# Expert matmuls of a two-layer MoE trunk: three fp32r passes over split weights, or plain float32 on 32-column tiles

## The chip, the cores and the metric

The kernel runs on one core of one Trainium2 chip. The metric is the device time of one execution in microseconds (us), the median of several runs.

## The reference, cut to what matters

A trunk of two layers over 512 tokens of width 1024. Each layer has a mixer (a state-space and pooling mixer in layer 0, a stick-breaking attention in layer 1), a layer norm, and then a mixture of 16 SwiGLU experts, of which each token uses two, beside a gated projection of an extra input:

```python
def grouped_moe(x, router_w, router_bias, w1, w3, w2):
    ...
    gates = jnp.sum(jax.nn.one_hot(idx, N_EXPERTS, dtype=F32) * w[..., None], axis=1)
    h = jax.nn.silu(jnp.einsum('td,edf->etf', xt, w1)) * jnp.einsum('td,edf->etf', xt, w3)
    h = h * gates.T[:, :, None].astype(h.dtype)
    y = jnp.einsum('etf,efd->td', h, w2)

def reference(...):
    for i in range(DEPTH):
        ...
        x = layer_norm(DEEPNORM_ALPHA * x + mix, ln_mix_g[i], ln_mix_b[i])
        ple = (p[i] @ ple_w_proj[i]) * jax.nn.sigmoid(x @ ple_w_gate[i])
        ffn = grouped_moe(x, router_w, router_bias, moe_w1[i], moe_w3[i], moe_w2[i])
        x = layer_norm(DEEPNORM_ALPHA * x + ffn + ple, ln_ffn_g[i], ln_ffn_b[i])
```

Per layer and expert, `w1` and `w3` are 1024 x 512 and `w2` is 512 x 1024, all float32.

## The kernel before, in words

The program runs in four stages: mixer 0, the expert layer 0, mixer 1 (attention), the expert layer 1. The change is in the expert layers, `ffn`, and in the helpers that load and split weights, which the mixers use too.

Each expert works on a list of at most 96 tokens (`CAP`). GpSimd gathers their rows from memory (`gather`, L936) and scatters the results back (`scatter`, L942). Per expert, six loads of 1 MB come through SP's queue (L107): two halves (of 512 rows) each of w1 and w3, and two halves (of 512 columns) of w2. `plan` lists all loads of the program in their order of use; `prefetch` issues them as far as `LA` loads ahead, into `NR` = 17 slots of 8 KB per partition (tag `raw`), which also hold the tokens `g`, the transposed activations and other tiles. A load puts row k*128 + p of the weights on partition p, so that each run of contiguous bytes is one row of 512 numbers, 2 KB.

A weight tile isn't multiplied as loaded. `weights` splits it (L84, L85): ScalarE copies a 128 x 1024 piece to the fp32r type as `w_0h` or `w_2h`, VectorE subtracts that copy from the original and gives `w_0l` or `w_2l`. These pairs live in a ring of 5 and 6 tiles. `mm3` then makes three matmuls for each product: high tokens with high weights (L89), high with low (L90), low with high (L91). The tokens (96 columns) are the stationary operand, 512 weight columns move. An expert has 24 such products, so 72 matmuls.

The order of an expert's work is written out in the loop over e. `up` for the next expert is cut in two halves of the contraction; between them stand the end of this expert and the load of the expert after the next one:

```python
            sg = act(hh)
            hh = [self.bank("A", "pA"), self.bank("A", "pA")]
            up(gn, hh, 0, 0)
            sT = turn(sg)
            up(gn, hh, 0, 1)
            ysb = self.half4("ysb")
            for h, py in down(sT):
                nc.scalar.activation(ysb[:CAP, h], py, AF.Copy)
            scatter(e, ysb)
```

`act` makes Silu on ScalarE (L1002) and the product on VectorE (L1003). `turn` transposes the result on TensorE (L1010) and splits it into `sT`. `down` multiplies by w2 into two PSUM banks `pB`, one after the other, and `load_g` transposes the tokens of a coming expert (L985) and splits them into `g`. After experts 3, 6 and 10 (`GATES`) a piece of the gated projection is put in. After the loop, the last expert's act, turn and down run with no other `up` beside them, and then each token's two results are added up by matmuls (L1068, L1071). A scheduler may move instructions of one engine against each other where their data allow it; the order of instructions that it leaves is shown below.

Of the kernel before, what the change touches and what calls it, by code (L numbers as in the profile page):

```python
# [7 lines left out]
F32 = mybir.dt.float32  # L8
F32R = mybir.dt.float32r
# [3 lines left out]
OP = mybir.AluOpType  # L13
# [5 lines left out]
KB = 8  # L19
# [1 line left out]
EPS = 1e-5  # L21
NE = 16
CAP = 96
NR = 17
RING = 6
NH = 5
GATES = (-1, 3, 6, 10)
OVER = 12
# [12 lines left out]
class Trunk:  # L41
# [51 lines left out]
    def plan(self, ap, k, n):  # L93
        self.queue.append((ap, k, n))
        return len(self.queue) - 1

    def prefetch(self, upto, parts=1):
        while self.loaded < min(upto, len(self.queue)):
            ap, k, n = self.queue[self.loaded]
            if k * n <= 512:  # L100
                t = self.sb.tile([128, 512], F32, tag="wp", bufs=1, name=f"raw{self.loaded}")
            else:
                t = self.slot(f"raw{self.loaded}")
            dst = t[:, :k * n].rearrange("p (k n) -> p k n", k=k)
            src = ap.rearrange("(k p) n -> p k n", p=128)
            for a in range(0, k, k // parts):
                self.nc.sync.dma_start(dst[:, a:a + k // parts], src[:, a:a + k // parts])  # L107
            self.raws[self.loaded] = t
            self.loaded += 1

    def weights(self, ahead, pool=False):
        i = self.used
        self.prefetch(i + 1 + ahead)
        self.used += 1
        ap, k, n = self.queue[i]
# [360 lines left out]
    def plain(self, ahead):  # L476
        i = self.used
        self.prefetch(i + 1 + ahead)
        self.used += 1
        ap, k, n = self.queue[i]  # L480
        return self.raws.pop(i)[:, :k * n].rearrange("p (k n) -> p k n", k=k)

    def mixer0(self):
# [433 lines left out]
    def ffn(self, layer, last):  # L917
# [34 lines left out]
            for k in range(2):  # L952
                self.mm3(p, (pT[:, 0, k, ts], pT[:, 1, k, ts]), w[k], k == 0, k == 1)

        LA = 6

        def gate(c):
            w = self.weights(LA, c < ng)
# [18 lines left out]
            gate(c)  # L977

        def load_g(e):
            g = self.slot(f"g{layer}_{e}", F32R)[:, :2 * KB * CAP].rearrange("p (a k t) -> p a k t", a=2, k=KB)  # L980
            for hf in range(2):
                p = self.bank("T", "pT")[:, :4 * CAP]
                for k in range(4):
                    kb = hf * 4 + k
# [21 lines left out]
        def turn(t):  # L1006
            sT = self.half4("sT", F32R)[:, :8 * CAP].rearrange("p (a k t) -> p a k t", a=2, k=4)
            p = self.bank("T", "pT")[:, :4 * CAP]
            for k in range(4):
                nc.tensor.transpose(p[:, k * CAP:(k + 1) * CAP], t[:CAP, k * 128:(k + 1) * 128], self.ident[:CAP, :CAP])  # L1010
            self.split(sT[:, 0], sT[:, 1], p.rearrange("p (k t) -> p k t", k=4))
            return sT

        def down(sT):
            for nh in range(2):
                w = self.weights(LA)
                py = self.bank("B", "pB")[:CAP]
                for k in range(4):
                    self.mm3(py, (sT[:, 0, k], sT[:, 1, k]), w[k], k == 0, k == 3)
                yield slice(nh * 512, (nh + 1) * 512), py  # L1020

        g = load_g(0)
        hh = [self.bank("A", "pA"), self.bank("A", "pA")]
        up(g, hh, 0, 0)
        up(g, hh, 0, 1)
        gn = load_g(1)
        up(g, hh, 1, 0)
        up(g, hh, 1, 1)
        for e in range(NE - 1):
            LA = 6 if e < 13 else 3  # L1030
            sg = act(hh)
            hh = [self.bank("A", "pA"), self.bank("A", "pA")]
# [17 lines left out]
            up(g, hh, 1, 0)  # L1050
            up(g, hh, 1, 1)
# [6 lines left out]
        for h, py in down(turn(act(hh))):  # L1058
            nc.scalar.activation(yl[:CAP, 0, h], py, AF.Copy, scale=self.gs[:CAP])
            v.scalar_tensor_tensor(yl[:CAP, 1, h], py, self.gs[:CAP], yl[:CAP, 0, h].bitcast(F32),  # L1060
                                   op0=OP.mult, op1=OP.subtract)
        st = self.cp.tile([128, NT, 12], F32, tag="st", bufs=2, name=f"st{layer}f")
        for i in range(NT):
# [129 lines left out]
    def plan_ffn(self, layer):  # L1193
# [7 lines left out]

        def up(e, kh):
            for n in ("moe_w1", "moe_w3"):
                self.plan(I[n][layer, e, kh * 512:(kh + 1) * 512, :], 4, 512)

        for c in range(GATES.count(-1)):
            gate(c)
# [2 lines left out]
        for e in range(NE):  # L1210
            if e + 1 < NE:
                up(e + 1, 0)
            for nh in range(2):
                self.plan(I["moe_w2"][layer, e, :, nh * 512:(nh + 1) * 512], 4, 512)
            if e in GATES:
                gate(GATES.index(e))
            if e + 1 < NE:
# [62 lines left out]
```

## Time and profile before

| | us |
|---|---|
| median of 3 runs | 1280.6 (1278.77 to 1281.57) |
| span of the profiled execution | 1278.0 |
| mixer 0 and routing, about 0 to 230 us of the span | 230 |
| expert layer 0, to the end of its loop | 230 to 550 |
| its end | 550 to 580 |
| mixer 1, routing | 580 to 900 |
| expert layer 1, its loop and its end | 900 to 1278 |

No time apart from the span is given for the profiled execution itself; the runs lie 0.8 to 3.6 us above the span, the median 2.6 us. A view in groups gives the busy time of each engine, a view in windows the same for stretches, the timeline every instruction in order, the waits what an engine waited for. The mean clock of TensorE over the span was 0.971 of full speed.

### The profile page before, as it was taken

What the parts mean: (1) busy time and instruction counts of PE and PEld (TensorE: products, weight loads), DVE (VectorE), ACT (ScalarE), POOL (GpSimd) and SP (SyncE); (2) the same over time, 40 slices, a digit from 0 to 9 for tenths busy, and PEclk for the clock granted to TensorE, in tenths of its full rate; (3) what the DMA queues carried; (4) which work ended last, traced back from release to release, by engine and by line L of the source; (5) the groups of instructions that cost most, each with busy time, mean ns of one, the idle gap of its engine ahead of it and who ended that gap; (6) DMA issues with size and microseconds to landing.
All of it is one profiled execution on the core that took longest, in us unless ns stands there. A gap on an engine that the chain in (4) does not pass through costs nothing. (4 is left out here: it accounts for less than half of the span.)

```text
span 1278.0 us, 17420 instructions
## 1 busy us (share of the span) xinstructions
PE 1191.0 (93%) x6511; PEld 910.8 (71%) x6511; DVE 982.7 (77%) x1358; ACT 748.4 (59%) x1043; POOL 180.5 (14%) x166
## 2 busy tenths in 40 slices
PE   6588998999999999997999999998999999999895
PEld 5467787778787786755877877787777778787662
DVE  7999678896969968766477376868797887969676
ACT  4123522886868868752465445612687786868761
POOL 5820031110000100003000000022111000010104
PEclk9888999999999999998999999998899999999898
DMA  8116463898998998971113023443599797999842
GB/s 236 58 50 211 153 229 123 278 365 304 339 340 303 365 337 317 344 273 34 34 32 101 1 67 121 161 148 124 189 353 373 266 370 275 364 340 356 314 189 89
DMA packets 158164, 285.12 MB, mean 223 GB/s; under 512 B 19584, under 2 KB 43664, under 8 KB 157008
## 3 DMA queue, kind: packets, MB, share of 16 engines
q1 hardware_dynamic: 143760, 256.56, 57.5%
q0 software_dynamic: 9568, 25.19, 5.8%
q10 hardware_dynamic: 4736, 2.10, 0.6%
q8 instruction: 55, 0.90, 0.3%
q14 instruction: 45, 0.37, 0.1%
HBM read 272.02 MB, written 20.19 MB: 229 GB/s over the span
## 5 line engine op out<-in xcount | busy, mean ns | idle before, releaser
L85 DVE TENSOR_TENSOR w_0l<-raw,w_0h 128x1024 fp32r<-128x1024 f32 (+1 forms) x231 | 281.3, 1219 | 68.2 <-ACT w_0h L84 59.8
L84 ACT ACTIVATE w_0h<-raw 128x1024 fp32r<-128x1024 f32 (+1 forms) x233 | 242.8, 1042 | 78.7 <-PE pG L91 37.8
L85 DVE TENSOR_TENSOR w_2l<-raw,w_2h 128x1024 fp32r<-128x1024 f32 x205 | 249.9, 1219 | 20.7 <-ACT w_2h L84 20.4
L84 ACT ACTIVATE w_2h<-raw 128x1024 fp32r<-128x1024 f32 x205 | 216.6, 1056 | 43.2 <-PE pA L91 34.1
L89 PE MATMUL pA<-w_0h,g 128*96 128x512 f32 x256 | 106.0, 414 | 0.0
L90 PE MATMUL pA<-w_0l,g 128*96 128x512 f32 x256 | 102.4, 400 | 0.0
L91 PE MATMUL pA<-w_2h,g 128*96 128x512 f32 x256 | 101.8, 398 | 0.0
L91 PE MATMUL pA<-w_0h,g 128*96 128x512 f32 x256 | 101.7, 397 | 0.0
L89 PE MATMUL pA<-w_2h,g 128*96 128x512 f32 x256 | 101.4, 396 | 0.0
L942 POOL DMA_INDIRECT yd<-ysb,ixm x30 | 32.2, 1075 | 488.1 <-ACT ysb L1038 488.1
L90 PE MATMUL pA<-w_2l,g 128*96 128x512 f32 x256 | 101.2, 395 | 0.0
L90 PEld LDWEIGHTS pA<-w_2l,g 128*96 128x96 f32 x256 | 41.8, 163 | 18.2
L91 PEld LDWEIGHTS pA<-w_0h,g 128*96 128x96 f32 x256 | 41.7, 163 | 17.9
L91 PEld LDWEIGHTS pA<-w_2h,g 128*96 128x96 f32 x256 | 41.6, 162 | 18.1
L89 PEld LDWEIGHTS pA<-w_2h,g 128*96 128x96 f32 x256 | 41.6, 163 | 18.0
L936 POOL DMA_INDIRECT xg<-xd,ixm x32 | 34.1, 1067 | 143.2 <-PE pT L985 98.6
L90 PEld LDWEIGHTS pA<-w_0l,g 128*96 128x96 f32 x256 | 42.4, 166 | 15.5 <-DVE w_0l L85 1.1
L89 PEld LDWEIGHTS pA<-w_0h,g 128*96 128x96 f32 x256 | 42.2, 165 | 14.5 <-ACT g L84 0.5
L89 PE MATMUL pB<-w_0h,sT 128*96 128x512 f32 x128 | 50.6, 396 | 1.2 <-ACT sT L84 1.2
L91 PE MATMUL pB<-w_0h,sT 128*96 128x512 f32 x128 | 51.4, 401 | 0.0
L90 PE MATMUL pB<-w_0l,sT 128*96 128x512 f32 x128 | 50.7, 396 | 0.4 <-DVE w_0l L85 0.4
L89 PE MATMUL pB<-w_2h,sT 128*96 128x512 f32 x128 | 50.8, 397 | 0.0
(439 smaller groups left out, 2918.5 us busy)
## 6 DMA issues: line engine op xcount, KB each, us to landing
raw<-in_moe_w_dram SPq DMA_DIRECT2D x192, 1024.0 KB
raw<-in_sb_w_qkv_dram SPq DMA_DIRECT2D x12, 1024.0 KB
raw<-in_ple_w_gate_dram SPq DMA_DIRECT2D x8, 1024.0 KB
yt<-yd SPq DMA_DIRECT2D x8, 1024.0 KB
raw<-in_ab_w_out_dram SPq DMA_DIRECT2D x4, 1024.0 KB
xd<-x0r POOLq DMA_DIRECT2D x8, 512.0 KB, 3.4
raw<-in_sb_w_out_dram SPq DMA_DIRECT2D x4, 1024.0 KB
raw<-in_ab_w_in_dram SPq DMA_DIRECT2D x3, 1024.0 KB
```

The lines of the kernel that those rows point to most:

```text
L84: return (self.nc.scalar.activation(hi, src, AF.Copy), (self.nc.gpsimd if pool else self.nc.vector).tensor_tensor(lo, src, hi.bitcast(F32) ...
L85: (self.nc.gpsimd if pool else self.nc.vector).tensor_tensor(lo, src, hi.bitcast(F32), op=OP.subtract))
L89: t.matmul(out, s[0], m[0], start=first, stop=False)
L90: t.matmul(out, s[0], m[1], start=False, stop=False)
L91: t.matmul(out, s[1], m[0], start=False, stop=last)
L936: return nc.gpsimd.indirect_dma_start(out=xgs[:CAP, e % 2, :], out_offset=None, in_=xd[:, :], in_offset=bass.IndirectOffsetOnAxis(ap=self. ...
L942: nc.gpsimd.indirect_dma_start(out=yd[:, :], out_offset=bass.IndirectOffsetOnAxis(ap=self.iy[:CAP, e:e + 1], axis=0), in_=src[:CAP], in_of ...
```

## The change

- The expert weights stay as loaded. The ring of split pairs is gone; gates and mixers, which still split their weights, put each pair in one slot of the `raw` tag (`ring_pair`), of which there are now 21.
- Loads of expert weights put several neighbouring rows on one partition (`rows`): four rows of w1 or w3, or two rows of w2 (which is now cut by rows, 256 x 1024), are 8 KB of contiguous bytes. The rows of a contraction are therefore permuted, and `load_g` and `turn` read their input with a stride of 4 or 2 columns, so that tokens and weights agree.
- `g` and `sT` are plain float32 and aren't split.
- Each expert matmul takes 32 tokens as its stationary operand and writes 32 PSUM partitions, at 0, 32, 64 or 96. In `up`, the four groups of partitions are w1 and w3 times two of the three token tiles; the third token tile has a bank of its own, where two parts of the contraction lie in different groups and are added later. `down` does the same with two column halves, and its third tile over two parts of the contraction. There are again 24 x 3 = 72 matmul instructions per expert.
- `act` is six operations instead of two, and the result of `down` is put together by two copies on ScalarE and a copy and two additions on VectorE, after all of `down`.
- Loads go 8 (later 5) ahead instead of 6 (3).

```diff
     def ring_pair(self, name):
-        h = self.sb.tile([128, 1024], F32R, tag="wh", bufs=RING - 1, name=name + "h")
-        l = self.sb.tile([128, 1024], F32R, tag="wl", bufs=RING, name=name + "l")
-        return h, l
+        t = self.slot(name, F32R)
+        return t[:, :1024], t[:, 1024:]
...
-            src = ap.rearrange("(k p) n -> p k n", p=128)
+            src = ap.rearrange("(p k) n -> p k n" if rows else "(k p) n -> p k n", p=128)
...
-        LA = 6
+        LA = 8
...
-                    nc.tensor.transpose(p[:, k * CAP:(k + 1) * CAP], xgs[:CAP, e % 2, kb * 128:(kb + 1) * 128],
-                                        self.ident[:CAP, :CAP])
-                ks = slice(hf * 4, hf * 4 + 4)
-                self.split(g[:, 0, ks], g[:, 1, ks], p.rearrange("p (k t) -> p k t", k=4))
+                    nc.tensor.transpose(p[:, k * CAP:(k + 1) * CAP],
+                                        xgs[:CAP, e % 2, hf * 512 + k:(hf + 1) * 512:4], self.ident[:CAP, :CAP])
...
-        def up(g, hh, kh, a, pool=False):
-            w = self.weights(LA, pool)
+        def up(g, hh, kh):
+            w = [self.plain(LA), self.plain(LA)]
+            mm = nc.tensor.matmul
             for k in range(4):
                 kb = kh * 4 + k
-                self.mm3(hh[a][:CAP], (g[:, 0, kb], g[:, 1, kb]), w[k], kb == 0, kb == KB - 1)
+                for a in range(2):
+                    for t in range(2):
+                        c = (2 * a + t) * 32
+                        mm(hh[0][c:c + 32], g[:, kb, t * 32:t * 32 + 32], w[a][:, k, :],
+                           start=(kb == 0), stop=(kb == KB - 1))
+            for k in range(2):
+                for s in range(2):
+                    for a in range(2):
+                        c = (2 * s + a) * 32
+                        q = k + 2 * s
+                        mm(hh[1][c:c + 32], g[:, kh * 4 + q, 64:96], w[a][:, q, :],
+                           start=(kh == 0 and k == 0), stop=(kh == 1 and k == 1))
 
         def act(hh):
             t = self.half4("sg")
-            sg = t[:CAP, :512]
-            nc.scalar.activation(sg, hh[0][:CAP], AF.Silu)
-            v.tensor_tensor(sg, sg, hh[1][:CAP], op=OP.mult)
-            return t
+            s = self.half4("ss")[:CAP, :512]
+            nc.scalar.activation(t[0:64, 512:], hh[1][64:128], AF.Copy)
+            nc.scalar.activation(t[64:128, :512], hh[0][0:64], AF.Silu)
+            v.tensor_tensor(t[0:64, 512:], t[0:64, 512:], hh[1][0:64], op=OP.add)
+            v.tensor_tensor(s[0:64], t[64:128, :512], hh[0][64:128], op=OP.mult)
+            nc.scalar.activation(t[32:64, :512], t[0:32, 512:], AF.Silu)
+            v.tensor_tensor(s[64:96], t[32:64, :512], t[32:64, 512:], op=OP.mult)
+            return s
...
         def down(sT):
+            mm = nc.tensor.matmul
+            py = [self.bank("B", "pB"), self.bank("B", "pB")]
+            for c in range(2):
+                w = self.plain(LA)
+                for k in range(2):
+                    kb = c * 2 + k
+                    for nh in range(2):
+                        for t in range(2):
+                            r = (2 * nh + t) * 32
+                            mm(py[0][r:r + 32], sT[:, kb, t * 32:t * 32 + 32], w[:, k, nh * 512:(nh + 1) * 512],
+                               start=(kb == 0), stop=(kb == 3))
+                for k in range(2):
+                    for nh in range(2):
+                        r = (2 * k + nh) * 32
+                        mm(py[1][r:r + 32], sT[:, c * 2 + k, 64:96], w[:, k, nh * 512:(nh + 1) * 512],
+                           start=(c == 0), stop=(c == 1))
...
         for e in range(NE - 1):
-            LA = 6 if e < 13 else 3
-            sg = act(hh)
-            hh = [self.bank("A", "pA"), self.bank("A", "pA")]
-            up(gn, hh, 0, 0)
-            sT = turn(sg)
-            up(gn, hh, 0, 1)
-            ysb = self.half4("ysb")
-            for h, py in down(sT):
-                nc.scalar.activation(ysb[:CAP, h], py, AF.Copy)
-            scatter(e, ysb)
+            LA = 8 if e < 13 else 5
+            ss = act(hh)
+            hh = banks()
+            up(gn, hh, 0)
+            scatter(e, down(turn(ss)))
```

On TensorE, before, around the transposes of an expert's activations (`sg`): `g_1` are the tokens of the next expert, `pA` its banks, `pB` the banks of `down`, the names of weights end in h or l.

```order
L91 MATMUL pA<-w_2h,g_1_1945 96x512
L1010 MATMUL pT<-ident,sg 128x96 x4
L89 MATMUL pA<-w_0h,g_1_1945 96x512
...
L91 MATMUL pA<-w_2h,g_1_1945 96x512
L89 MATMUL pB<-w_0h,sT 96x512
L90 MATMUL pB<-w_0l,sT 96x512
```

Twelve matmuls of the next expert stand between the transposes and the first matmul that reads `sT`. At the same place of the program now (L1027 are these transposes, L982 those of `load_g`, L1001 and L1008 `up`, L1041 and L1046 `down`; `raw` are the weights as loaded):

```order
L1008 MATMUL pA<-raw_2055,g_3_2166 32x512
L1027 MATMUL pT<-ident,ss 128x96 x4
L982 MATMUL pT<-ident,xg_1478 128x96 x4
L1001 MATMUL pA<-raw_2128,g_3_2166 32x512
L1041 MATMUL pB<-raw_2091,sT 32x512 x8
L1046 MATMUL pB<-raw_2091,sT 32x512 x4
L1041 MATMUL pB<-raw_2093,sT 32x512 x8
L1046 MATMUL pB<-raw_2093,sT 32x512 x4
L982 MATMUL pT<-ident,xg_1478 128x96 x4
L1001 MATMUL pA<-raw_2128,g_3_2166 32x512
L1001 MATMUL pA<-raw_2142,g_3_2166 32x512 x2
```

All 24 matmuls of `up`'s first half now stand ahead of the transposes; between the transposes and `down` stand four of `load_g`'s eight transposes and a single matmul of 32 columns, and the other four transposes follow `down`.

On VectorE, before, the stretch from the product of one expert (L1003) to the tokens of a coming one (`g_3`):

```order
L1003 TENSOR_TENSOR sg<-sg,pA 96x512
L85 TENSOR_TENSOR w_0l<-raw_2063,w_0h 128x1024
L85 TENSOR_TENSOR w_2l<-raw_2063,w_2h 128x1024
L85 TENSOR_TENSOR w_0l<-raw_2087,w_0h 128x1024
L85 TENSOR_TENSOR sT<-pT,sT 128x384
L85 TENSOR_TENSOR w_2l<-raw_2087,w_2h 128x1024
```

And one expert's work on VectorE now:

```order
L1017 TENSOR_TENSOR ss<-sg,pA 64x512
L1016 TENSOR_TENSOR sg<-sg,pA 64x512
L1019 TENSOR_TENSOR ss<-sg 32x512
L1028 COPY sT<-pT 128x384
L986 COPY g_3_2166<-pT 128x384
L1055 TENSOR_TENSOR ysb<-yt,pB 32x512
L1052 COPY ysb<-pB 64x512
L1055 TENSOR_TENSOR ysb<-yt,pB 32x512
```

The subtractions for the weights are gone, the product has become three operations in a chain, `sT` is a copy that no longer waits for ScalarE's half of a split, and three operations for the result of `down` have come to VectorE.

## Rows read from the trace of the kernel before

**Rows 1.** Page: busy time of engines, share of the span, instructions.

```profile
PE 1191.0 (93%) x6511; PEld 910.8 (71%) x6511; DVE 982.7 (77%) x1358; ACT 748.4 (59%) x1043; POOL 180.5 (14%) x166
```

**Rows 2.** Windows: length, busy PE, PEld, DVE, ACT, POOL; clock, DMA share, GB/s.

```profile
230.00:550.00 320.00, 317.05 (x1674) 238.48 (x1673) 262.81 (x278) 252.10 (x308) 30.81 (x30) 1.00 0.93 328
580.00:900.00 320.00, 306.00 (x1721) 240.91 (x1722) 211.33 (x369) 141.72 (x290) 24.74 (x19) 0.98 0.24 82
340.00:376.00 36.00, 36.00 (x194) 27.47 (x193) 28.94 (x29) 27.42 (x33) 3.01 (x3) 1.00 1.05 373
```

**Rows 3.** Waits of PE, 225 to 550 us: all there are.

```profile
PE pT L985 <- PEq L1105: 3.0, 1, 3.0
```

**Rows 4.** Timeline of PE, one expert: start, length, instructions.

```profile
342.96 0.49 PE L1010 MATMUL pT<-ident,sg 96*128 96x96 f32 x4
343.24 0.45 PE L89 MATMUL pA<-w_0h,g 128*96 128x512 f32 x1
343.53 0.39 PE L90 MATMUL pA<-w_0l,g 128*96 128x512 f32 x1
...
351.63 0.82 PE L985 MATMUL pT<-ident,xg 96*128 96x96 f32 x8
352.24 0.45 PE L89 MATMUL pA<-w_0h,g 128*96 128x512 f32 x1
...
360.64 0.49 PE L1010 MATMUL pT<-ident,sg 96*128 96x96 f32 x4
```

**Rows 5.** Timeline of PE at plain float32 matmuls with 128 columns (two windows).

```profile
560.30 7.03 PE L1068 MATMUL pA<-yt,dg 128*128 128x512 f32 x16
560.73 1.45 PE L1068 MATMUL pA<-yt,dg 128*128 128x512 f32 x3
```

**Rows 6.** Timeline of PE in mixer 0: 32-column tiles.

```profile
90.29 1.96 PE L422 MATMUL pT<-s5M,s5x 128*32 128x128 f32 x64
92.17 0.50 PE L89 MATMUL pA<-x0Th,w_0h 128*128 128x512 f32 x1
92.51 0.39 PE L90 MATMUL pA<-x0Tl,w_0h 128*128 128x512 f32 x1
```

**Rows 7.** Timeline of PE in mixer 0: 64-column tiles beside full ones.

```profile
118.14 0.44 PE L568 MATMUL pB<-s5T,U 128*64 128x128 f32 x4
118.36 0.44 PE L569 MATMUL pB<-s5M,St 128*64 128x128 f32 x4
118.73 0.71 PE L468 MATMUL pA<-band,vp 128*128 128x128 f32 x4
...
129.66 0.39 PE L91 MATMUL pA<-w_2h,catl 128*128 128x512 f32 x1
129.97 0.45 PE L568 MATMUL pB<-s5T,U 128*64 128x128 f32 x4
```

**Rows 8.** Timeline, an expert's transposes and the copy of `sT`; brackets: idle before.

```profile
537.53 0.49 PE L1010 MATMUL pT<-ident,sg 96*128 96x96 f32 x4
...
538.07 0.49 ACT L84 ACTIVATE sT<-pT 128x384 fp32r<-128x384 f32 x1 [1.99 <-PE pT L1010]
```

**Rows 9.** Timeline of PE at the end of layer 0's experts.

```profile
552.83 0.55 PE L1010 MATMUL pT<-ident,sg 96*128 96x96 f32 x4 [0.78 <-DVE sg L1003]
553.96 0.47 PE L89 MATMUL pB<-w_0h,sT 128*96 128x512 f32 x1 [0.58 <-ACT sT L84]
```

**Rows 10.** Groups of VectorE and ScalarE: busy, mean ns, idle before.

```profile
L1003 DVE TENSOR_TENSOR sg<-sg,pA 96x512 f32<-96x512 f32 x11 | 7.5, 680 | 2.8 <-PE pA L91 2.8
L1002 ACT ACTIVATE sg<-pA 96x512 f32<-96x512 f32 x12 | 7.2, 596 | 2.0 <-PE pA L91 1.9
```

**Rows 11.** Timeline of PE in mixer 0: transposes of neighbouring and of every 16th column.

```profile
9.34 1.97 PE L170 MATMUL pT<-ident,x 128*128 128x128 f32 x8 [0.78 <-ACT s5sm L237]
...
20.00 1.15 PE L275 MATMUL pT<-ident,s5in 64*128 64x64 f32 x8
```

**Rows 12.** Waits of SP's queue, 225 to 550 us: the largest.

```profile
SPq L107 <- DVE w_2l L85: 203.8, 56, 34.7
```

More of the change, by code (lines that the diff above doesn't have):

```diff
@@ L23 @@
 CAP = 96
-NR = 17
-RING = 6
+NR = 21
 NH = 5
@@ L91, in mm3, with plan @@
         t.matmul(out, s[1], m[0], start=False, stop=last)
-    def plan(self, ap, k, n):
-        self.queue.append((ap, k, n))
+    def plan(self, ap, k, n, rows=False):
+        self.queue.append((ap, k, n, rows))
         return len(self.queue) - 1
@@ L98, in prefetch @@
         while self.loaded < min(upto, len(self.queue)):
-            ap, k, n = self.queue[self.loaded]
+            ap, k, n, rows = self.queue[self.loaded]
             if k * n <= 512:
@@ L114, in weights @@
         self.used += 1
-        ap, k, n = self.queue[i]
+        ap, k, n, _ = self.queue[i]
         raw = self.raws.pop(i)
@@ L479, in plain @@
         self.used += 1
-        ap, k, n = self.queue[i]
+        ap, k, n, _ = self.queue[i]
         return self.raws.pop(i)[:, :k * n].rearrange("p (k n) -> p k n", k=k)
@@ L979, in load_g @@
         def load_g(e):
-            g = self.slot(f"g{layer}_{e}", F32R)[:, :2 * KB * CAP].rearrange("p (a k t) -> p a k t", a=2, k=KB)
+            g = self.sb.tile([128, KB, CAP], F32, tag="g", bufs=3, name=f"g{layer}_{e}")
             for hf in range(2):
@@ L1008, in turn @@
+            v.tensor_tensor(t[0:64, 512:], t[0:64, 512:], hh[1][0:64], op=OP.add)
[3 more added lines that the diff above has]
+            return s
+        def turn(s):
+            sT = self.half4("sT")[:, :4 * CAP].rearrange("p (k t) -> p k t", k=4)
             p = self.bank("T", "pT")[:, :4 * CAP]
@@ L1009, in turn @@
             for k in range(4):
-                nc.tensor.transpose(p[:, k * CAP:(k + 1) * CAP], t[:CAP, k * 128:(k + 1) * 128], self.ident[:CAP, :CAP])
-            self.split(sT[:, 0], sT[:, 1], p.rearrange("p (k t) -> p k t", k=4))
+                c = k // 2 * 256
+                nc.tensor.transpose(p[:, k * CAP:(k + 1) * CAP], s[:, c + k % 2:c + 256:2], self.ident[:CAP, :CAP])
+            v.tensor_copy(sT.rearrange("p k t -> p (k t)"), p)
             return sT
         def down(sT):
-            for nh in range(2):
[L1016 to L1020, printed above, removed]
+            mm = nc.tensor.matmul
@@ new lines, in down, with banks @@
+            y = self.half4("ysb")
+            t = self.half4("yt")
+            nc.scalar.activation(t[0:64, :512], py[1][64:128], AF.Copy)
+            nc.scalar.activation(y[0:64, :512], py[0][0:64], AF.Copy)
+            v.tensor_copy(y[0:64, 512:], py[0][64:128])
+            for nh in range(2):
+                r = slice(nh * 32, nh * 32 + 32)
+                v.tensor_tensor(y[64:96, nh * 512:(nh + 1) * 512], t[r, :512], py[1][r], op=OP.add)
+            return y
+        def banks():
+            return [self.bank("A", "pA"), self.bank("A", "pA")]
@@ L1022, in ffn @@
         g = load_g(0)
-        hh = [self.bank("A", "pA"), self.bank("A", "pA")]
-        up(g, hh, 0, 0)
-        up(g, hh, 0, 1)
+        hh = banks()
+        up(g, hh, 0)
         gn = load_g(1)
-        up(g, hh, 1, 0)
-        up(g, hh, 1, 1)
+        up(g, hh, 1)
         for e in range(NE - 1):
-            LA = 6 if e < 13 else 3
-            sg = act(hh)
-            hh = [self.bank("A", "pA"), self.bank("A", "pA")]
-            up(gn, hh, 0, 0)
-            sT = turn(sg)
-            up(gn, hh, 0, 1)
-            ysb = self.half4("ysb")
-            for h, py in down(sT):
-                nc.scalar.activation(ysb[:CAP, h], py, AF.Copy)
-            scatter(e, ysb)
+            LA = 8 if e < 13 else 5
+            ss = act(hh)
+            hh = banks()
+            up(gn, hh, 0)
+            scatter(e, down(turn(ss)))
@@ L1049, in ffn @@
                 gn = load_g(e + 2)
-            up(g, hh, 1, 0)
-            up(g, hh, 1, 1)
+            up(g, hh, 1)
         yts = []
@@ L1057, in ffn @@
         yl = self.slot(f"yl{layer}", F32R).rearrange("p (a d) -> p a d", a=2)
-        for h, py in down(turn(act(hh))):
-            nc.scalar.activation(yl[:CAP, 0, h], py, AF.Copy, scale=self.gs[:CAP])
-            v.scalar_tensor_tensor(yl[:CAP, 1, h], py, self.gs[:CAP], yl[:CAP, 0, h].bitcast(F32),
+        y = down(turn(act(hh)))[:CAP]
+        for nh in range(2):
+            h = slice(nh * 512, (nh + 1) * 512)
+            nc.scalar.activation(yl[:CAP, 0, h], y[:, h], AF.Copy, scale=self.gs[:CAP])
+            v.scalar_tensor_tensor(yl[:CAP, 1, h], y[:, h], self.gs[:CAP], yl[:CAP, 0, h].bitcast(F32),
                                    op0=OP.mult, op1=OP.subtract)
@@ L1203, in up @@
             for n in ("moe_w1", "moe_w3"):
-                self.plan(I[n][layer, e, kh * 512:(kh + 1) * 512, :], 4, 512)
+                self.plan(I[n][layer, e, kh * 512:(kh + 1) * 512, :], 4, 512, True)
         for c in range(GATES.count(-1)):
@@ L1212, in plan_ffn @@
                 up(e + 1, 0)
-            for nh in range(2):
-                self.plan(I["moe_w2"][layer, e, :, nh * 512:(nh + 1) * 512], 4, 512)
+            for c in range(2):
+                self.plan(I["moe_w2"][layer, e, c * 256:(c + 1) * 256, :], 2, 1024, True)
             if e in GATES:
```

8 lines of the change are left out of this document (5 added, 3 removed).

## The prediction

> **What bounds the kernel now.** I read the totals first, then windows by stage, then the waits of the engine that looks fullest. TensorE is busy 93% of the span, VectorE 77% and ScalarE 59% [rows 1]; this mean over four different stages doesn't say what an expert waits for. In the window of layer 0's experts TensorE is busy 317.05 of 320 us at a granted clock of 1.00, VectorE 262.81 and ScalarE 252.10 [rows 2]. All waiting of TensorE from 225 to 550 us is one branch of 3.0 us [rows 3]: no weight, split or load is ever late there. So the expert loops, over 600 us of the span, last as long as TensorE's own instructions, and the splitting on the other two engines, however busy it keeps them, delays nothing.
>
> The timeline gives an expert's parts. From one set of transposes to the next it is 360.64 - 342.96 = 17.68 us [rows 4]. Between 343.53 and 351.63 lie 35 matmuls, 8.10/35 = 0.2314 us each, so 72 take 16.66 us; the 12 transposes, with what they lose at their edges, take the other 1.02 us.
>
> **The change, part by part: the matmuls.** What does a plain float32 matmul cost, and do four narrow ones run side by side? The trace has both apart. L1068 is plain float32, 512 columns moving: 16 records last 7.03 us and 3 last 1.45, so one record costs (7.03 - 1.45)/13 = 0.429 us [rows 5], and the program has two records for each such matmul. L422 writes four groups of 32 partitions in turn, 128 columns each: 64 records start at 90.29 and the next instruction at 92.17 [rows 6], 0.0294 us each. A record of 128 columns would cost 0.429/4 = 0.107 alone; four side by side would be 0.027. So four do run together, within 10%. Seventy-two matmuls in fours are 18 steps of two records: 18 x 2 x 0.429 = 15.44 us instead of 16.66, a gain of 1.22 per expert, 39.0 for 32 experts. A single column group at a time would be four times 15.44; rows 6 exclude that for this shape.
>
> **Changing between narrow and full matmuls.** An expert goes from narrow tiles to full-width transposes and back twice (the four `load_g` transposes behind `turn`, and the four behind `down`): four switches. Rows near it: L569 to L468 takes 0.37 us where four such records take 0.22, so 0.15 more; L91 to L568 takes 0.31 instead of 0.23, 0.08 more [rows 7]; L89 behind L422 takes 92.51 - 92.17 = 0.34 instead of 0.23, 0.11 more [rows 6]. I take 0.13 each, 0.52 per expert, between 0 and 0.6. The Trainium skill speaks against the change here: "TensorEngine Tiling (Array Packing)", Tiling Modes, Key Properties, says that changing the tiling mode drains the engine. It gives no time; the rows above show a loss at each such change, and of this size.
>
> **The single matmul ahead of `down`.** Before, twelve matmuls of the next expert hid the copy of `sT`. Now four transposes (0.33) and one matmul of 32 columns do. `sT` is ready late: the copy starts 0.54 us after the first transpose starts and takes 0.49 [rows 8], so some 1.1 us after it, and without the stray matmul TensorE would wait about 0.45. With it, nothing is waited for, but it fills one column group for 2 x 0.429 = 0.86 us while three stand empty, and the first matmul of `down` wants the same group. When `up` goes on later, its other three groups still need all their steps. So I charge 0.86 whole; its bounds are 0 (others start past it) and 0.9. It happens in 15 experts per layer, 30 times.
>
> **The transposes.** They now read every 4th or 2nd column. L275 reads every 16th: 8 of 64 columns in 1.15 us, where L170 in the same stretch does 8 of 128 neighbouring columns in 1.97 [rows 11]. Half of that is 0.98, so stride costs at most 0.17/8 = 0.02 each, 0 to 0.25 per expert. I take 0.
>
> **The end of each layer.** There nothing hides `act`. Before, TensorE waited 0.78 for the product and 0.58 for `sT` [rows 9]. Now Silu and product of 64 rows can run while the third token tile still accumulates, but behind the last matmul come a copy and a Silu on ScalarE (0.6 each by L1002) and an addition and a product on VectorE (0.68 each by L1003) [rows 10] in one chain, 2.55 instead of 0.68: +1.9 per layer, +3.8 in all. If the copy and additions hide, +1. The result of this `down` is put together by more steps too, but L1068 runs for 7 us there without needing it [rows 5].
>
> **What I cost at nothing.** The splits removed: their cover is that TensorE never waits for them [rows 3]; they would gain only if TensorE's time fell below theirs. The longer `act` in the loop: 24 matmuls of `up` (6 steps, 5.1 us) lie over it. `down`'s result, which holds both `pB` banks until the last addition: the next `down` comes ten or more us later. Loads: contiguous 8 KB pieces and a deeper lead can only cure waits for data, and there are none; SP's queue waits for slots, 203.8 us behind the splits [rows 12], so loads run as far ahead as slots allow. Attention's order changes, since its fill no longer waits for a ring; TensorE was idle 14 us of 320 there [rows 2]. I take 0, with a fifth of that either way, 3 us.
>
> **Sum.** Per looped expert 15.44 + 1.02 + 0.52 + 0.86 = 17.84, against 17.68. In all: -39.0 + 30 x (0.52 + 0.86) + 3.8 = +6.2 us on the span of 1278.0, so 1284.2; the median lay 2.6 above that span: 1287 us.
>
> **Rivals.**
> - *Faster: the stray matmul or the switches hide.* If the groups run past each other and the stray costs nothing, the sum is -39.0 + 15.6 + 3.8 = -19.6: 1261 us. With switches free as well it is -35.2: 1245. For it: tiles that write different partitions do overlap [rows 6]. Against: all three pairs of rows on a switch show a loss, and `down` starts in the stray's own group. It decides at 35.2/30 = 1.17 us of extra time per expert; I have 1.38, so this is close.
> - *Four tiles don't overlap fully at 512 columns.* Two at a time would be 30.9 us per expert, some 1780 us in all; rows 7 have pairs of 64-column tiles at 0.055 per record, rows 6 speak against it. Milder: three groups' worth of speed, as if one of the four always stood: 15.44/0.75 = 20.6 us, +5.1 for each of 32: 1452. L422 reaches 0.107/4 in 0.0294, 0.91 of the ideal with its switch included [rows 6]. The Trainium skill's "TensorE: Matmul & The Clock Gate", Part 3: Packing small matmuls, gives a measured 2.38 times for three column tiles with 512 columns, 0.79 of the ideal, which would make 15.44/0.79 = 19.5 us of an expert's matmuls and 1418 us of the whole.
> - *Weights come late.* An expert needs 6.3 MB of weights and some 0.8 MB of gathered and scattered rows, 7.1 MB; at the 373 GB/s of the window 340 to 376 [rows 2] that is 19.0 us, more than 17.84. Gates and the lead make it up today (328 GB/s over the layer). If they no longer do, 1.16 us in some 26 experts is +30: 1317. That slots also hold the split pairs now speaks for it, eight loads' lead and 105 MB in 320 us against it.
> - *Attention loses its fill*, or slots run short in the mixers, and its 14 us of idle TensorE [rows 2] nearly double: about +12, 1299.
>
> **How the numbers follow.** My forecast 0.45; faster rival 0.32; weights late 0.08; attention 0.08; tiles at three groups' speed 0.04, pairs 0.03. From no change this kernel can be told at about 0.2%, 2.6 us: the forecast's own range is 1272 to 1304 (switches 0.45 to 0.6, stray 0.7 to 0.9, stride 0 to 0.25, attention 3 either way), which puts about a tenth of the chance each below 1278 and between 1278 and 1283.2. So faster 0.37, same 0.12, slower 0.51. The range reaches down to between the two values of the faster rival, 1252, and up to weights late, 1318; below it lie some 0.08, above it the tiles that don't overlap and a part of the late weights, 0.11.
>
> **What would show it.** L1001, L1008, L1041 and L1046 at 8 records per 0.858 us (right), or more (tiles don't overlap). A gap of 0.86 us between the single L1001 and the first L1041: right; L1041 in another group starting at once: the faster rival. Each step from L1008 to L1027 and back some 0.13 us longer than its cadence. From one L1027 to the next 17.8 us without a gate. No wait of TensorE for a DMA in the loops; if there is one, the weights are late. At the end of each layer, L1027 waits some 2.5 us for the last product. I am wrong if the period is under 17.5 us: then the overheads that I read off mixer 0 don't carry over.

## The result, and the profile after

The changed kernel takes 1347.14 us (1346.89 to 1350.21) where the kernel before takes 1280.6 beside it (1278.77 to 1281.57; a fourth execution of 2960.14 us is left out): 1.0529 times as long, 95% interval 1.0507 to 1.0552. I had forecast 1287 and a range up to 1318. Its profiled span is 1348.5 us against 1278.0, 70.5 us more.

The page's line of engines shows VectorE and ScalarE relieved as meant (982.7 and 748.4 before [rows 1]), TensorE not:

```profile
PE 1226.7 (91%) x8815; PEld 739.3 (55%) x8815; DVE 640.1 (47%) x1104; ACT 382.2 (28%) x661; POOL 170.6 (13%) x166
```

The timeline of TensorE over one expert, which answers to [rows 4]:

```profile
361.91 0.72 PE L1027 MATMUL pT<-ident,ss 96*128 96x96 f32 x4
362.47 0.64 PE L982 MATMUL pT<-ident,xg 96*128 96x96 f32 x4
363.04 0.62 PE L1001 MATMUL pA<-raw,g 128*32 128x512 f32 x1
363.33 0.63 PE L1041 MATMUL pB<-raw,sT 128*32 128x512 f32 x3
363.50 0.59 PE L1001 MATMUL pA<-raw,g 128*32 128x512 f32 x1
363.79 1.59 PE L1041 MATMUL pB<-raw,sT 128*32 128x512 f32 x12
365.07 0.61 PE L1046 MATMUL pB<-raw,sT 128*32 128x512 f32 x3
365.21 0.59 PE L1041 MATMUL pB<-raw,sT 128*32 128x512 f32 x1
...
368.08 1.16 PE L1046 MATMUL pB<-raw,sT 128*32 128x512 f32 x5
369.17 0.72 PE L982 MATMUL pT<-ident,xg 96*128 96x96 f32 x4
369.82 3.21 PE L1001 MATMUL pA<-raw,g 128*32 128x512 f32 x27
...
380.25 0.72 PE L1027 MATMUL pT<-ident,ss 96*128 96x96 f32 x4
```

The period is 380.25 - 361.91 = 18.34 us, where I had worked out 17.84 and the kernel before has 17.68. The four transposes of `ss` take 0.56 us to the next instruction; before, four took 0.28 [rows 4].

The span falls apart at instructions that both kernels have: the last matmul of the token lists (L912, now L910) ends routing, and the transposes of the activations (L1010, now L1027) mark the experts. Lengths of the stages in us, from the timelines (the forecast for the stretch from the first to the last expert is 15 periods of 0.16, less the 1.22 saved on the one expert whose matmuls lie before and behind them):

| stage | before | after | difference | forecast |
|---|---|---|---|---|
| mixer 0 and routing | 217.0 | 225.3 | +8.3 | 0 |
| from there to the first expert's transposes, layer 0 | 23.1 | 29.9 | +6.8 | 0 |
| from the first to the last expert's, layer 0 | 312.7 | 330.4 | +17.7 | +1.2 |
| layer 0's end, mixer 1, routing | 344.0 | 361.0 | +17.0 | +1.9 |
| to the first expert's transposes, layer 1 | 24.6 | 29.9 | +5.3 | 0 |
| from the first to the last expert's, layer 1 | 316.5 | 329.5 | +13.0 | +1.2 |
| layer 1's end | 40.0 | 42.5 | +2.5 | +1.9 |

Over half of the loss, 39.9 us, lies outside the expert loops or at their ends, where I had expected 3.8. The waits of TensorE over the whole run say where to look (total, times, longest); in the kernel before the same waits were 5.9, 4.5 and 1.0 us, none listed, 1.7, 0.4 and 1.6 (where the third has its longest wait, TensorE waited 4.2 for something else before):

```profile
PE pT L982 <- PEq L1138: 8.2, 2, 4.8
PE pT L982 <- DMA xg<-xd,ixm: 8.1, 3, 3.9
PE pT L168 <- DVE x2Tl L83: 7.8, 3, 6.3
PE pA L87 <- ACT w L82: 7.3, 5, 1.7
PE pB L671 <- ACT kw L677: 7.1, 11, 2.6
PE pA L89 <- DVE w L83: 6.0, 1, 6.0
PE pT L1027 <- DVE ss L1019: 5.8, 2, 2.9
```

Two of them are weights' splits of the mixers (`w`, L82 and L83), one is attention (L671), one the first gather of a layer (`xg`), and the first stands behind the overflow test (L1138). Windows around that gather, with the clock and the DMA share behind the busy times:

```profile
228.00:234.00 6.00, 2.68 (x23) 2.47 (x21) 0.69 (x1) 0.60 (x1) 1.23 (x2) 0.99 0.83 268
234.00:236.00 2.00, 1.46 (x8) 1.26 (x8) 0.00 (x0) 0.49 (x1) 0.00 (x0) 0.50 0.99 393
236.00:242.00 6.00, 6.00 (x37) 1.55 (x40) 1.23 (x3) 0.00 (x0) 1.94 (x2) 0.61 0.83 305
```

While weights are loaded at 268 GB/s the gather lands 3.86 us after TensorE has run out of work; TensorE then works at a granted clock of 0.50 (1.2 GHz) and 0.61, and the first 32 narrow matmul records last 5.94 us instead of 3.6 (worked out from 0.429 for each four). Before, the same gather landed 2.18 us late and the clock from 224 to 230 us was 0.77, so only a part of this is new.

### The profile page after: what moved, and what is told of

Same layout as the page of the kernel before. It is cut to its first block, busy times and chain, and to the rows that moved or that the text cites. A ratio compares the mean times of both kernels' runs of the same rounds, so it can differ in the third digit from the quotient of the medians.

```text
span 1348.5 us, 21035 instructions
## 1 busy us (share of the span) xinstructions
PE 1226.7 (91%) x8815; PEld 739.3 (55%) x8815; DVE 640.1 (47%) x1104; ACT 382.2 (28%) x661; POOL 170.6 (13%) x166
## 5 line engine op out<-in xcount | busy, mean ns | idle before, releaser
L1001 PE MATMUL pA<-raw,g 128*32 128x512 f32 x2048 | 295.9, 611 | 0.0
L1008 PE MATMUL pA<-raw,g 128*32 128x512 f32 x1024 | 169.7, 593 | 0.0
L1041 PE MATMUL pB<-raw,sT 128*32 128x512 f32 x1024 | 153.4, 609 | 1.4 <-issue 1.4
L1001 PEld LDWEIGHTS pA<-raw,g 128*32 128x32 f32 x2048 | 77.0, 112 | 140.2 <-issue 130.5
L1046 PE MATMUL pB<-raw,sT 128*32 128x512 f32 x512 | 95.8, 605 | 0.0
L82 ACT ACTIVATE w<-raw 128x1024 fp32r<-128x1024 f32 (+1 forms) x74 | 72.4, 1010 | 75.1 <-PE pA L89 55.2
L83 DVE TENSOR_TENSOR w<-raw,w 128x1024 fp32r<-128x1024 f32 (+1 forms) x70 | 79.9, 1159 | 18.8 <-ACT w L82 18.3
L1041 PEld LDWEIGHTS pB<-raw,sT 128*32 128x32 f32 x1024 | 49.2, 111 | 67.0 <-issue 61.9
L1008 PEld LDWEIGHTS pA<-raw,g 128*32 128x32 f32 x1024 | 44.3, 110 | 70.5 <-issue 68.1
L982 PE MATMUL pT<-ident,xg 96*128 96x96 f32 x256 | 43.8, 301 | 20.8 <-PEq L1138 8.2
L982 PEld LDWEIGHTS pT<-ident,xg 96*128 96x128 f32 x256 | 36.3, 216 | 46.7 <-issue 28.5
L87 PE MATMUL pA<-x2Th,w 128*128 128x512 f32 x128 | 51.1, 399 | 2.3 <-ACT w L82 2.3
L988 ACT ACTIVATE g<-pT 128x384 f32<-128x384 f32 x32 | 15.7, 490 | 127.3 <-PE pT L982 127.1
L679 DVE TENSOR_TENSOR_SCAN kw<-kw 128x128 f32<-128x128 f32 (+3 forms) x64 | 50.3, 812 | 2.3 <-ACT kw L676 2.0
L88 PE MATMUL pA<-x2Tl,w 128*128 128x512 f32 x128 | 50.6, 395 | 0.0
```

Source lines behind the costliest of these rows:

```text
L82: return (self.nc.scalar.activation(hi, src, AF.Copy), (self.nc.gpsimd if pool else self.nc.vector).tensor_tensor(lo, src, hi.bitcast(F32) ...
L83: (self.nc.gpsimd if pool else self.nc.vector).tensor_tensor(lo, src, hi.bitcast(F32), op=OP.subtract))
L87: t.matmul(out, s[0], m[0], start=first, stop=False)
L679: v.tensor_tensor_scan(rv, rv, rv, 1.0, op0=OP.mult, op1=OP.min)
L1001: mm(hh[0][c:c + 32], g[:, kb, t * 32:t * 32 + 32], w[a][:, k, :], start=(kb == 0), stop=(kb == KB - 1))
L1008: mm(hh[1][c:c + 32], g[:, kh * 4 + q, 64:96], w[a][:, q, :], start=(kh == 0 and k == 0), stop=(kh == 1 and k == 1))
```

## The experiments

Ratios are to the kernel before on the same chip, with their 95% intervals. "Period" is the distance from one expert's transposes to the next where no gate stands between them.

**Contiguous transposes.** `contig_only`:

```diff
-                                        xgs[:CAP, e % 2, hf * 512 + k:(hf + 1) * 512:4], self.ident[:CAP, :CAP])
+                                        xgs[:CAP, e % 2, (hf * 4 + k) * 128:(hf * 4 + k + 1) * 128], self.ident[:CAP, :CAP])
...
-                nc.tensor.transpose(p[:, k * CAP:(k + 1) * CAP], s[:, c + k % 2:c + 256:2], self.ident[:CAP, :CAP])
+                nc.tensor.transpose(p[:, k * CAP:(k + 1) * CAP], s[:, k * 128:(k + 1) * 128], self.ident[:CAP, :CAP])
```

> The changed kernel with the transposes of tokens and activations reading neighbouring columns instead of every 4th or 2nd one; the weights are still loaded with neighbouring rows on a partition, so products pair the wrong rows. Theory (the stride makes the transposes slow): the 120 ns from one transpose to the next fall back to about 82 ns, the expert period from 18.34 to about 17.85 us, the whole by 32 x 0.48 = 15 us to about 1332. Rival (transposes are slow because they stand between narrow matmuls): spacing stays at 120 ns and the time at 1347.

1335.95 us, 1.0437 (1.0411 to 1.0464); period 17.85. It was the stride. The transposes of the tokens (loads of the stationary operand, then matmuls; shortest, median, longest ns, first and last start), first in the changed kernel, then here:

```profile
L982 PEld LDWEIGHTS pT<-ident,xg x256: 194/218/231, 234.5 to 1284.8; 96*128 96x128 f32 x128
L982 PE MATMUL pT<-ident,xg x256: 282/284/412, 234.5 to 1284.9; 96*128 96x96 f32 x128
```

```profile
L982 PEld LDWEIGHTS pT<-ident,xg x256: 138/141/231, 235.1 to 1271.0; 96*128 96x128 f32 x128
L982 PE MATMUL pT<-ident,xg x256: 246/246/395, 235.1 to 1271.1; 96*128 96x96 f32 x128
```

The tokens are the operand that is loaded as weights in a transpose, and that load takes 218 ns with the stride and 141 without.

**Loads as before as well.** `contig_rows_off`: the same, and `(k p) n -> p k n` for all loads.

> The changed kernel with transposes of neighbouring columns and, to match them, the weights loaded with row k*128 + p on partition p again, in pieces of 2 KB (4 KB for w2). Theory (TensorE bounds the loops, the layout of the loads is worth nothing there): same time as the run with neighbouring columns alone, about 1332 us. Rival (the 8 KB pieces bring the weights sooner and the loops need it): loads late, waits of TensorE for DMA in the loops, 5 us or more above that run.

1341.63 us, 1.0479 (1.0452 to 1.0506). In the loops the period is 17.85 again and TensorE waits for no weights; but each layer's stretch from routing to the first expert is 33.6 and 33.2 us instead of 29.7 and 29.1. The 8 KB pieces are worth nothing in the loops and, with the shared slots, some 4 us at each start. With a ring that gain isn't seen: `all_18_4` (2 KB pieces) and `ring_split_up` (8 KB), both below, have starts of 22.9 and 23.6 in layer 0.

**A ring of their own for the split pairs.** `ring`:

```diff
-NR = 21
+NR = 16
+RING = 6
...
-        t = self.slot(name, F32R)
-        return t[:, :1024], t[:, 1024:]
+        h = self.sb.tile([128, 1024], F32R, tag="wh", bufs=RING - 1, name=name + "h")
+        l = self.sb.tile([128, 1024], F32R, tag="wl", bufs=RING, name=name + "l")
+        return h, l
```

> The changed kernel with the split pairs of mixers and gates in a ring of their own again (5 and 6 tiles) and 16 slots instead of 21; everything else as changed. Theory (the shared slots and the deeper lead cost the time outside the loops): the delay of mixer 0 and its norm (8.2 us), that of routing to the first expert (6.8 and 5.3 us) and that of attention (15.3 us) go for the most part, 20 to 35 us less, 1312 to 1327 us, with the period in the loops still 18.34 us. Rival (the delays come from an order that the scheduler chose for other reasons): within 5 us of 1347.

1309.59 us, 1.0239 (1.0215 to 1.0263), 37.6 us less than the changed kernel. Mixer 0 to routing takes 217.4 us, the starts of the layers 25.3 and 25.0, the stretch with attention 339.6: all near the kernel before; the period stays at 18.34. This is the largest part of the loss. In the stretch with attention 13.5 of the 21.3 us that come back are idle time of TensorE (28.6 us there in the changed kernel, 15.2 here); the rest is the same work at a granted clock of 0.98 instead of 0.96.

**The same part alone, in the kernel before.** `before_shared`: the kernel before with that edit the other way round (21 slots, no ring).

> The kernel before with one part of the change alone: the ring is gone, split pairs take slots, of which there are 21; loads, expert matmuls and lead as before. The expert loops split every weight and are short of slots now, so only the stages of the mixers are to be compared. Theory (sharing alone delays the mixers): the end of routing in layer 0 at about 225 us instead of 217, the stretch from the last expert of layer 0 to routing in layer 1 about 361 us instead of 344. Rival (the delay needs the rest of the change): 217 and 344 within 3 us.

1384.78 us, 1.0813 (1.0786 to 1.0841); its loops are slower too (341 and 342 us instead of 313 and 317), which isn't the question here. Mixer 0 to routing takes 227.2 us, the starts 29.5 and 29.3, the stretch with attention 370.5 (which holds layer 0's slower end). Sharing alone does it: TensorE waits 6.9 us in 11 waits for `kw` in attention (7.1 in 11 in the changed kernel), and the wait in mixer 0 is the one of the changed kernel (6.0 us there), in the window 70 to 90 us:

```profile
PE pA L89 <- DVE w L83: 6.1, 1, 6.1
```

VectorE around that wait in the changed kernel, and the first product behind it:

```profile
75.68 2.38 DVE L333 TENSOR_TENSOR s5Bs<-s5Bs,s5td 128x1024 f32<-128x1024 f32 x2
...
79.52 1.22 DVE L83 TENSOR_TENSOR w<-raw,w 128x1024 fp32r<-128x1024 f32 x1
...
80.79 0.80 PE L89 MATMUL pA<-x0Th,w 128*128 128x512 f32 x1 [6.04 <-DVE w L83]
```

VectorE doesn't stand idle before this split; it works through the mixer's own operations first. In the kernel before the two low halves of this stretch are made ahead of those operations, at 42.96 and 55.98 us, in `ring` at 42.67 and 55.70, in `before_shared` at 78.98 and 80.31. So with shared slots the split lands later in VectorE's order.

**Fewer slots; a shorter lead.** `slots19` and `lead6`:

```diff
-NR = 21
+NR = 19
```

```diff
-        LA = 8
+        LA = 6
...
-            LA = 8 if e < 13 else 5
+            LA = 6 if e < 13 else 3
```

> The changed kernel with 19 shared slots instead of 21. If the lack of slots makes the splits of mixers late: mixer 0 beyond 225.3 us to the end of routing and attention beyond 361 us, 5 to 20 us in all, loops at 18.34 as long as the lead holds. If the number of slots isn't the cause: within 4 us of 1347.

> The changed kernel with loads 6 and later 3 ahead as before, 21 shared slots and everything else as changed. If the deeper lead takes slots or bandwidth from mixers and gathers: a good part of the 37.6 us comes back, under 1335 us, with the first gather of each layer no longer 3.6 to 3.9 us late. If the split pairs in shared slots do it: 1347 within 4 us, loop period 18.34.

19 slots: 1376.74 us, 1.0767 (1.0746 to 1.0788). Mixer 0 loses 5.6 us more and the starts go from 29.9 to 40.3 and 40.0, but the stretch with attention is 358.1, no worse than with 21. The shorter lead: 1348.14 us, 1.054 (1.0518 to 1.0562), no stage more than 0.9 us from the changed kernel. So it isn't the lead; fewer slots make the loss in mixer 0 and at the starts larger. Attention went against what I expected of `slots19`: what of sharing hurts it, if not the number of slots, these runs don't show.

**No single matmul ahead of `down`.** `split_up`:

```diff
-            up(gn, hh, 0)
-            scatter(e, down(turn(ss)))
+            w = up0(gn, hh, 0)
+            sT = turn(ss)
+            up1(gn, hh, 0, w)
+            scatter(e, down(sT))
```

`up0` is the part of `up` that writes `hh[0]`, `up1` the part that writes `hh[1]`.

> The changed kernel with the first half of up cut in two: its 16 matmuls of the first two token tiles ahead of the transposes of the activations, its 8 of the third tile behind them, as cover for the copy of sT; no single matmul stands ahead of down, and the eight transposes of the tokens stand together behind down. Theory (the single matmul with the wait for sT costs 0.88 us per expert): period 17.46 us instead of 18.34, 30 x 0.88 = 26 us less, 1321 us. Rival (other column groups work past the single matmul and it costs nothing): period 18.3, 1347 us.

1325.77 us, 1.036 (1.0334 to 1.0386); period 17.51, 0.83 less. The timeline of TensorE has the transposes, eight covering matmuls (two records each) and `down` without a gap:

```profile
356.76 0.72 PE L1034 MATMUL pT<-ident,ss 96*128 96x96 f32 x4
357.41 1.92 PE L1015 MATMUL pA<-raw,g 128*32 128x512 f32 x16
359.15 1.90 PE L1048 MATMUL pB<-raw,sT 128*32 128x512 f32 x16
```

**Stride alone, in the kernel before.** `before_strided`: the two strided reads put into the kernel before.

> The kernel before with the transposes of tokens and activations reading every 4th and every 2nd column, as in the change; weights stay as they were, so products pair the wrong rows. If stride alone costs 0.04 us per transpose, wherever it stands: the period rises from 17.68 by 12 x 0.04 = 0.48 to 18.16 us and the whole by 15 us to 1294. If it shows only beside narrow plain float32 matmuls: 17.68 and 1279.

1292.02 us, 1.0104 (1.0083 to 1.0125); period 18.06, 0.38 more than 17.68. The stride costs by itself; between narrow matmuls 12 transposes cost 0.49 for it.

**All three remedies, and fewer changes between narrow and full.** `all` joins `ring`, `split_up` and `contig_rows_off`; `lg_early` is `all` with `load_g` in banks of `pB`, called right behind `turn` (against `all`):

```diff
             sT = turn(ss)
-            up1(gn, hh, 0, w)
+            g = gn
+            if e + 2 < NE:
+                gn = load_g(e + 2, "B")
+            up1(g, hh, 0, w)
...
-            g = gn
-            if e + 2 < NE:
-                gn = load_g(e + 2)
```

> The changed kernel with three of its parts undone or altered at once: the ring of split pairs with 16 slots, up cut in two around the transposes of the activations, and transposes of neighbouring columns with weights loaded as before. If the three add up: 1347 - 37.6 (ring) - 21.4 (cut up) - 5.5 (columns and loads) = 1282.6 us, the period in the loops 18.34 - 0.83 - 0.49 = 17.02 us against 17.68 before, so the loops alone would be faster than before by 6 us each where there is no gate, and what is left over lies at the overflow test and the layers' ends. Rival (they share a cost): more than 1295.

> The run with all three, and the eight transposes of the coming tokens put right behind those of the activations, in banks of tag B: two changes between narrow and full matmuls per expert instead of four. Theory (each change costs about 0.13 us): the period falls from 17.02 to 16.76, 30 x 0.26 = 8 us less. Rival (what is lost at a change is the latency of the first full matmuls, and goes with the number of transposes): the same period. If the banks of tag B are late for down, the period rises by up to 0.5.

`all`: 1295.34 us, 1.0148 (1.0126 to 1.017), period 17.02. `lg_early`: 1300.68, 1.0176 (1.0158 to 1.0194), period 16.73. Both periods are as worked out, and two changes fewer gave 0.29, 0.145 each; both totals are misses, 13 us above what the sum of the three gave and 5 us more instead of 8 less. Periods with a gate (a piece of the gated projection) are 33.1 to 36.2 and 34.5 to 39.9 us. VectorE around one of them in `all`:

```profile
295.50 1.23 DVE L85 TENSOR_TENSOR w_0l<-raw,w_0h 128x1024 fp32r<-128x1024 f32 x1 [4.21 <-ACT w_0h L84]
296.64 0.55 DVE L1037 COPY sT<-pT 128x384 f32<-128x384 f32 x1
```

The copy of `sT` stands behind a split that waits for the gate's weights, which land late (ScalarE waits 3.83 us for them ahead of its half): loads run at 375 GB/s there, while an expert in 17.02 us wants 7.1 MB, 417 GB/s.

**More slots, or the gates' splits elsewhere?** `all_18_4` and `lge_18_4` are `all` and `lg_early` with 18 slots and a ring of 3 and 4; `ring_split_up` has that ring, `split_up`, strided transposes and 8 KB pieces.

> The run with all three, with 18 slots and a ring of 3 and 4 tiles instead of 16 slots and 5 and 6. In that run gate weights came late (a period with a gate of 35.6 to 36.2 us where 17.02 + 14.4 = 31.4 would do), with TensorE waiting for a copy of sT that stood behind a split of the late weights. Theory (at 17.02 us per expert the loads, at 375 GB/s, no longer keep up, and the slots set how long the lead lasts): two slots more, 2 MB or 5 us of loading, make gate periods 32 to 34 us, 10 to 20 us less, 1275 to 1285 us; mixers may lose a few us by the smaller ring. Rival (the order on VectorE alone does it): gate periods unchanged.

> The run with the tokens' transposes behind those of the activations, with 18 slots and a ring of 3 and 4 tiles. Period 16.73 us as with 16 slots; gate periods, 38 to 40 us with 16 slots, fall to 33 to 36 by the same theory: 1300 - 15 to 25 = 1275 to 1285 us.

> The changed kernel (8 KB pieces, strided transposes) with 18 slots, a ring of 3 and 4 tiles and up cut in two. Period 17.51 us as with up cut in two. If the loads are what is late at gates, here, with longer pieces and a slower pace, gates show no wait for sT and take 33 us: 1348 - 21.4 - 37.6 = 1288 us. If a gate takes 35 us or more all the same, it is the order on VectorE.

1299.57 (1.0133 to 1.0177), 1317.2 (1.0277 to 1.0329) and 1306.38 us (1.0187 to 1.0225): all three miss the 1275 to 1288 that I expected. In their traces the smaller ring costs mixer 0 seven to ten us and the attention stretch eight to eleven (226.8 and 351.1 in `all_18_4`), more than the loops gain; by the runs' medians `all_18_4` is level with `all`. At a period of 17.51 gates show no wait for `sT` and take 33.38 us.

`all_pool` puts the low halves of the gates' splits on GpSimd; `all_pool_17_5` has 17 slots and a ring of 4 and 5 as well:

```diff
-            w = self.weights(LA, c < ng)
-            wp = self.weights(LA)
+            w = self.weights(LA, True)
+            wp = self.weights(LA, True)
```

> The run with all three, with the low half of the gates' weight splits on GpSimd instead of VectorE, so that VectorE's copy of sT no longer stands behind a split that waits for late gate weights. If that order costs the 5.5 us of waits for sT and a like amount behind it in layer 0: gate periods 36 to about 33 us, 15 to 20 us less over both layers, 1275 to 1280 us, level with the kernel before. If the late weights themselves cost it: TensorE waits for them at the gate instead, 1295.

> The same with 17 slots and a ring of 4 and 5 tiles: loops 2 to 4 us better than with 16 slots if slots set the lead, mixers up to 8 us worse if the smaller ring delays their splits.

`all_pool`: 1281.08 us, 1.0009 (0.9989 to 1.0028), level with the kernel before: the order on VectorE had cost 14 us. `all_pool_17_5`: 1313.24, 1.0255 (1.0233 to 1.0276), a miss: its mixers are fine (215.8 and 345.0), but the last ungated period ahead of each gate is 18.5 to 23.1 us long instead of 17.02. In layer 0 TensorE waits 16.6 us there for the product of `act`, in four waits (7.8 in two in `all_pool`). At the longest, ScalarE waits 4.01 us for the gate's weights, since its half of their split stands ahead of a copy that `act` needs:

```profile
289.45 1.06 ACT L84 ACTIVATE w_0h<-raw 128x1024 fp32r<-128x1024 f32 x1 [4.01 <-DMA raw<-in_ple_w_gate_dram]
290.42 1.04 ACT L84 ACTIVATE w_4h<-raw 128x1024 fp32r<-128x1024 f32 x1
291.48 0.59 ACT L1023 ACTIVATE sg<-pA 64x512 f32<-64x512 f32 x1
```

Why this is worse than in `all_pool`, where the same order costs less, isn't shown.

`all_pool_hi` and `lge_pool_hi` put the high halves of the gates' splits on GpSimd too (`gpsimd.tensor_copy`).

> The run with the low half of the gates' splits on GpSimd, with the high half there too (a copy instead of ScalarE's). TensorE still waited 7.8 us in layer 0 for a product whose Silu stood behind a split of late gate weights on ScalarE; if that wait goes and nothing new comes, 2 x 5 to 8 us less: 1266 to 1272 us, ahead of the kernel before by 0.6 to 1%. Rival (GpSimd is slow at the copies and the gate waits for them): 1281 or more.

> The same with the tokens' transposes behind those of the activations (two changes between narrow and full matmuls instead of four): period 16.73 us instead of 17.02, another 8 us less than the run beside it if loads keep up, 0 to 10 us more if the faster pace only brings waits for late loads.

`all_pool_hi`: 1268.39 us, 0.9913 (0.9899 to 0.9926), every gate period at 32.89 us. `lge_pool_hi`: 1259.58 us (1255.39 to 1265.09), 0.9846 (0.9819 to 0.9872), faster than both kernels. Its window 230 to 550 us holds two thirds less work on VectorE and ScalarE than [rows 2] at nearly the same load of TensorE and DMA:

```profile
230.00:550.00 320.00, 312.60 (x2800) 134.16 (x2803) 95.96 (x154) 75.96 (x122) 53.68 (x48) 1.00 0.95 343
```

## Why the prediction was wrong

**Bound and matmuls: right.** The expert loops are bound by TensorE's own instructions in both kernels, and removing the splits gained nothing. Four narrow float32 matmuls run together: 12 records in the 1.28 us from 363.79 to 365.07 in the timeline above, four in 0.427, so 15.4 us per expert. The four-tile rivals fell. The 2.38 times that the Trainium skill's "TensorE: Matmul & The Clock Gate", Part 3: Packing small matmuls, gives for three column tiles, 0.79 of the ideal, isn't what this trace shows with four.

**Changes between narrow and full: right.** I took 0.13 each; `lg_early` against `all` gives 0.145. The Trainium skill's "TensorEngine Tiling (Array Packing)", Tiling Modes, Key Properties, says that a change of tiling mode drains the engine; the loss at each change here agrees with that, though no run shows the drain itself.

**The single matmul: right in price, not in form.** I charged 0.86; `split_up` gives 0.83. I had expected `down` to wait 0.86 behind it. Three matmuls of `down` in other column groups start 0.29 us after it, at 363.33, and what they wait for is `sT`, whose copy ends 0.1 us before them:

```profile
362.67 0.56 DVE L1028 COPY sT<-pT 128x384 f32<-128x384 f32 x1 [3.07 <-PE pT L1027]
```

In `contig_only` they start 0.44 us after the single matmul, and again 0.1 after that copy. The group that the single matmul holds then trails to the end of `down`, where its last record starts 0.55 us after those of the other three (368.65 against 368.09). The 0.29 at the front and the 0.55 at the end are the 0.84 for which three groups stand empty. So the price came right for the reason given, three groups that stand empty, but the gap of 0.86 that I named as its sign didn't appear.

**The transposes: mis-sized.** "I take 0", between 0 and 0.25 per expert, was 0.49: 15.7 us by 32 experts, 11 us in the medians of `contig_only` and the changed kernel. I priced the stride by L275 against half of L170's spacing [rows 11]. That half, 0.12 us, was itself longer than the 0.08 of the transposes in question [rows 4], L275 has another shape (64 rows, 64 columns), and what the stride lengthens, the load of the stationary operand from 141 to 218 ns, I left out. With 0.49 put in for 0, the sum per expert is 18.33 against 18.34 measured.

**What I cost at nothing: the step that failed.** "Attention's order changes ... I take 0, with a fifth of that either way, 3 us", and mixer 0 wasn't in the sum at all. The shared slots cost 37.6 us. My rival "slots run short in the mixers" named the thing, but I gave it 0.08 and 12 us, from TensorE's idle time in attention alone. `ring` takes the loss away, `before_shared` makes it alone, `slots19` makes it larger outside attention.

**The ends of the layers: right.** TensorE waits 2.9 us for the last product, where I had 2.55, and layer 1's end is 2.5 us longer instead of 1.9.

**What was left out.** The overflow test behind expert 12: the two periods around it rose from 21.29 and 20.75 to 27.36 and 23.08 in layer 0, and from 25.07 and 20.77 to 26.44 and 23.08 in layer 1, 12.1 us together, of which 2.6 are the 0.66 that every period gained. TensorE's waits behind the branch for the transposes of the next tokens rose from 5.9 and 1.1 us to 8.2 and 4.5. Gates: 33.39 - 18.34 = 15.05 us instead of 14.40, 0.65 six times. No run took the branch apart, or the gates. The shared slots (37.6), the stride (15.7), the branch (9.5) and the gates (3.9) make 66.7 us, about the 64.3 by which the forecast missed the span.

## What to carry to other kernels

When a change lets two kinds of tiles share one tag, the price can be paid far from where the change was made: go through every stage that uses the tag, and look what its tiles will now wait for. A stride has to be priced on the operand that it lies on, with rows of the same shape. And where faster matmuls make loads late, look at what stands behind the late data in the queues of other engines: moving the gates' weight splits to GpSimd turned 1.0148 into 0.9913.

## What the runs showed of the hardware that I had not expected

- A transpose whose input is read with a stride of 4 float32 columns loads it in 218 ns instead of 141 (96 x 128, L982 in the changed kernel and in `contig_only`), with a stride of 2 in 216 (L1027), and one follows the other in 0.12 us instead of 0.08.
- A single narrow matmul holds up only its own column group: matmuls of the other three started 0.29 us after it, as soon as their operand was there, though it held its group for two records of 0.43. The loss of 0.83 us came all the same, 0.29 at the front and the rest by a trailing group at the end.
- A wait of 3.86 us for a gather was followed by a granted clock of 0.50 and 0.61 over the next 8 us, so that it cost over 6 us in all (an estimate: 3.86 and 5.94 - 3.6).
